# A fixed order, a PE run-up and later small loads for the first product of a decoder trunk

## The chip, the cores and the metric

The kernel runs on one core of one Trainium2 chip. The core has five engines that work side by side: TensorE (PE), which multiplies matrices and transposes tiles; VectorE (DVE); ScalarE (ACT); GpSimd (POOL); and SyncE (SP), which here only issues loads and stores. SyncE and ACT each have a DMA queue, and both share the core's 16 DMA engines. The metric is the device time of one execution in microseconds (us). The time before is the median of three runs.

## The reference

One layer of a hybrid decoder trunk on 256 tokens of 2048 channels in float32: a norm, one combined input projection, two token mixers side by side (a gated delta rule and a causal pooling), gates, an output projection, and a gated MLP with a causal convolution. What matters here is its beginning:

```
h = rmsnorm(x, norm_mix_w)                 # x: 256 x 2048
proj = h @ w_in                            # 2048 x 14368
q, k, v, z, b_raw, a_raw, p_in, g_a, g_b = split(proj)
qkv = silu(causal_dwconv(concat(q, k, v), conv_qkv_w))
```

The rest (delta rule, pooling, `w_out`, `w_up`, `w_down`, final norm) is not touched by the change.

## The kernel before

**Precision.** Every large product is done in three matmuls on split operands. ACT casts a float32 tile to the rounded type (`hi`), VectorE takes what is left (`lo`), and PE adds up hi x hi, lo x hi and hi x lo. The activations are the stationary operand, the weights the moving one.

**Weights.** `srcs` lists all weight tiles in the order of use, each 128 x 1024 (two blocks of 128 rows by 512 columns, 512 KB). `begin(n)` prepares tiles up to number n: a load on SyncE into one of four `raw` buffers (L110), the cast `whi` on ACT (L112), the rest `wlo` on VectorE (L119); `whi` and `wlo` have three buffers each. `weights()` prepares `AHEAD` = 2 tiles beyond the one that it hands out.

**Products.** `gemm_a` runs over the 8 weight tiles of a product (2048 rows). For each it does 12 matmuls, 128 x 128 by 128 x 512: two blocks, two halves of the tokens, three parts, at L149 (`xhi` with `whi`), L150 (`xlo` with `whi`) and L151 (`xhi` with `wlo`).

**The beginning.** x comes in four quarters `x0[c]` of 512 channels (L218), each followed by two weight tiles. The rows of `norm_mix_w` (`nmrows`) are turned on PE (L225) and copied to `nmw`. Then PE turns x in 128 x 128 blocks (L234, 8 transposes a quarter), and each turned block is scaled by `nmw` and split by ACT (`xhi`, L238) and VectorE (`xlo`, L239). The first product (`ps_k0`, the keys of the first heads) follows. The row norms of x are taken by squares on ACT (L311, 8 of 128 x 512) and are only needed when a product is evicted (L457). After the first product comes the small product for beta and decay (L362).

**Small loads.** ACT's queue loads `nmrows`, `vrows`, `cqrows`, `cfrows`, `alb`, `dtb`, `gwb`, `psb`, and writes four small blocks of zeros (L450). SyncE's queue loads the four `taps` of the value convolution (L466), which VectorE first reads at L476. The pooling bands are built on POOL and finished on VectorE by 8 subtractions (L430).

**Order.** The order of instructions on each engine is not written out: a planner lists them by priority (the order in the text) and by the time at which a simulated timeline has their inputs ready. Each engine then executes its list strictly in that order. Every DMA signals a semaphore when it has landed; there are eight of them in turn, over both queues, so an issue waits until the load that had the same semaphore before has landed.

```
 99     def weights():
101         begin(taken[0] + AHEAD + 1)
...
220         begin(2 * c + 2)
...
248     ps_k0 = gemm_a(xh, xl, KD)
```

Of the kernel before, what the change touches and what calls it, by code (L numbers as in the profile page):

```python
# [7 lines left out]
F32 = mybir.dt.float32  # L8
F32R = mybir.dt.float32r
I32 = mybir.dt.int32  # L10
AF = mybir.ActivationFunctionType
ALU = mybir.AluOpType

P = 128
S = 256
D = 2048
NH = 16
KD = D // P
DFF = 5632
KF = DFF // P  # L20
# [4 lines left out]
C_Q, C_K, C_V, C_Z = 0, 2048, 4096, 6144  # L25
# [3 lines left out]
AHEAD = 2  # L29
# [4 lines left out]
def kernel(  # L34
# [20 lines left out]
    nc = tc.nc  # L55
    mm = nc.tensor.matmul

    cpool = ctx.enter_context(tc.tile_pool(name="cpool", bufs=1))
    big = ctx.enter_context(tc.tile_pool(name="big", bufs=1))
    wpool = ctx.enter_context(tc.tile_pool(name="wpool", bufs=3))  # L60
# [6 lines left out]
    def nm(s):  # L67
        cnt[0] += 1
        return f"{s}_{cnt[0]}"

    def pg(shape=(P, 512)):
        return psg.tile(list(shape), F32, tag="g", name=nm("psg"))
# [6 lines left out]
    srcs = []  # L79
# [16 lines left out]
    made = []  # L96
    taken = [0]

    def weights():

        begin(taken[0] + AHEAD + 1)
        taken[0] += 1
        return made[taken[0] - 1]

    def begin(n):
        while len(made) < min(len(srcs), n):
            src = srcs[len(made)]
            shape = list(src.shape)
            raw = wpool.tile(shape, F32, tag="raw", name=nm("raw"), bufs=4)
            nc.sync.dma_start(raw, src)  # L110
            hi = wpool.tile(shape, F32R, tag="whi", name=nm("whi"))
            nc.scalar.copy(hi, raw)  # L112
            if shape[1] == 8:
                lo = None
                nc.vector.tensor_tensor(hi[:, :, 32:64], raw[:, :, 0:32], hi[:, :, 0:32].bitcast(F32),
                                        op=ALU.subtract)
            else:
                lo = wpool.tile(shape, F32R, tag="wlo", name=nm("wlo"))
                nc.vector.tensor_tensor(lo, raw, hi.bitcast(F32), op=ALU.subtract)  # L119
            made.append((hi, lo))  # L120
# [11 lines left out]
    def pm():  # L132
        return psm.tile([P, 2, 512], F32, tag="m", name=nm("psm"))
# [4 lines left out]
    def gemm_a(lh, ll, nk, steps=None, ps=None):  # L138

        ps = pm() if ps is None else ps  # L140
        for c in range(nk // 2) if steps is None else steps:
            if c == 1:
                while later:
                    later.pop(0)()
            hi, lo = weights()
            for kk in range(2):
                k = 2 * c + kk
                for t in range(2):
                    mm(ps[:, t, :], lh(k, t), hi[:, kk, :], start=(k == 0), stop=False)  # L149
                    mm(ps[:, t, :], ll(k, t), hi[:, kk, :], start=False, stop=False)  # L150
                    mm(ps[:, t, :], lh(k, t), lo[:, kk, :], start=False, stop=(k == nk - 1))  # L151
                side()
        return ps
# [45 lines left out]
    ones = cpool.tile([P, P], F32, name="ones")  # L199
    nc.gpsimd.memset(ones, 1.0)  # L200
    ident = cpool.tile([P, P], F32, name="ident")
# [2 lines left out]
    epsx = cpool.tile([P, 2], F32, name="epsx")  # L204
    nc.gpsimd.memset(epsx, -0.5)

    def mtile(i, shape, dt, name):
        return big.tile(shape, dt, tag=f"m{i}", name=name)

    mix = tc.tile_pool(name="mix", bufs=1)  # L210
    mp = mix.__enter__()

    nmrows = mp.tile([KD, P], F32, tag="w1", name="nmrows")
    nc.scalar.dma_start(nmrows, norm_mix_w[0].rearrange("(r p) -> r p", p=P))
    x0 = []
    for c in range(4):
        xc = mtile(c, [P, 2, 512], F32, f"x0_{c}")
        nc.sync.dma_start(xc, x[0, :, c * 512 : (c + 1) * 512].rearrange("(t p) d -> p t d", p=P))  # L218
        x0.append(xc)
        begin(2 * c + 2)  # L220


    nmw = cpool.tile([P, KD], F32, name="nmw")
    pv = pg()
    nc.tensor.transpose(pv[:, :KD], nmrows, ident[:KD, :KD])  # L225
    nc.vector.tensor_copy(nmw, pv[:, :KD])
    xhl = big.tile([P, KD, 2, S], F32R, tag="xhl", name="xhl")
    xhi, xlo = xhl[:, :, 0, :], xhl[:, :, 1, :]
    for k2 in range(KD // 2):
        pt = pg([P, 2, S])  # L230
        for kk in range(2):
            k = 2 * k2 + kk
            for t in range(2):
                nc.tensor.transpose(pt[:, kk, t * P : (t + 1) * P], x0[k // 4][:, t, (k % 4) * P : (k % 4 + 1) * P],  # L234
                                    ident)
        for kk in range(2):
            k = 2 * k2 + kk
            nc.scalar.activation(xhi[:, k, :], pt[:, kk, :], AF.Copy, scale=nmw[:, k : k + 1])  # L238
            nc.vector.scalar_tensor_tensor(xlo[:, k, :], pt[:, kk, :], nmw[:, k : k + 1], xhi[:, k, :].bitcast(F32),  # L239
                                           op0=ALU.mult, op1=ALU.subtract)  # L240

    def xh(k, t):
        return xhi[:, k, t * P : (t + 1) * P]
# [1 line left out]
    def xl(k, t):  # L245
        return xlo[:, k, t * P : (t + 1) * P]

    ps_k0 = gemm_a(xh, xl, KD)


    NV = 16 + KF
    V_FFN, V_CB = 0, 16
    vrows = mp.tile([NV, P], F32, tag="th", name="vrows")
    for off, n, src in ((V_FFN, 16, norm_ffn_w), (V_CB, KF, conv_ffn_b)):
        nc.scalar.dma_start(vrows[off : off + n, :], src[0].rearrange("(r p) -> r p", p=P))
    cqrows = mp.tile([96, 2, P], F32, tag="cy", bufs=2, name="cqrows")
    nc.scalar.dma_start(cqrows, conv_qkv_w.rearrange("o j (r p) -> (o j r) p", p=P)
                        .rearrange("(a q) p -> q a p", a=2))
    cfrows = mp.tile([66, 2, P], F32, tag="cy", bufs=2, name="cfrows")
    nc.scalar.dma_start(cfrows, conv_ffn_w.rearrange("o j (r p) -> (o j r) p", p=P)  # L260
                        .rearrange("(a q) p -> q a p", a=2))
    alb = cpool.tile([P, NH], F32, name="alb")
    nc.scalar.dma_start(alb, a_log[0].partition_broadcast(P))
    dtb = cpool.tile([P, NH], F32, name="dtb")
    nc.scalar.dma_start(dtb, dt_bias[0].partition_broadcast(P))

    vec = cpool.tile([P, NV], F32, name="vec")
    pv = pg()
# [3 lines left out]
    pv = pg()  # L272
# [4 lines left out]
    pv = pg()  # L277
# [3 lines left out]

    def scales(g):
        psb = mp.tile([P, 512], F32, tag="psb", name=nm("psb"))
        nc.scalar.dma_start(psb, pool_scale[0, 512 * g : 512 * g + 512].partition_broadcast(P))
        return psb

    gwb = mp.tile([P, P], F32, name="gwb")
    nc.scalar.dma_start(gwb, gdn_norm_w[0].partition_broadcast(P))

    def rstd_rows(ssq, dst):  # L290

# [12 lines left out]
        nc.vector.tensor_copy(dst, pr[:, :S])  # L304
        return rs

    ssq4 = cpool.tile([P, 2, 4], F32, tag="ssq4", name="ssq4a")
    for c in range(4):
        for t in range(2):
            junk = cpool.tile([P, 512], F32, tag="sqj", name=nm("junk"))  # L310
            nc.scalar.activation(junk, x0[c][:, t, :], AF.Square, accum_out=ssq4[:, t, c : c + 1])  # L311
    ssq = cpool.tile([P, 2], F32, name="ssq")
    nc.vector.tensor_reduce(ssq, ssq4, axis=mybir.AxisListType.X, op=ALU.add)
    rs1 = rstd_rows(ssq, None)
# [34 lines left out]
    idh = mp.tile([P, P], F32, name="idh")  # L349
# [8 lines left out]
    for c in range(2):  # L358
        hi, lo = weights()
        for kk in range(8):  # L360
            k = 8 * c + kk
# [57 lines left out]
    for g, win in enumerate(WINDOWS):  # L419
        bd = bands[:, g, :]  # L420
        nc.gpsimd.memset(bd, 0.5 / win)
        nc.vector.tensor_copy(bd[:, 0:PAD], icnt[:, g, :])
        for cs in (slice(0, P + PAD), slice(P + PAD, NB)):
            b = bd[:, cs]
            n = cs.stop - cs.start
            nc.gpsimd.affine_select(b, b, pattern=[[1, n]], compare_op=ALU.is_ge, fill=0.0, base=0,
                                    channel_multiplier=-1)
            nc.gpsimd.affine_select(b, b, pattern=[[-1, n]], compare_op=ALU.is_ge, fill=0.0, base=win - 1,
                                    channel_multiplier=1)
            nc.vector.tensor_tensor(b[:, 0:P], b[:, 0:P], idh, op=ALU.subtract)  # L430


    Ta = mp.tile([P, 8, P], F32, name="T")
# [11 lines left out]
    SH = 3  # L445
    vrow = dpool.tile([4, SH + S, 512], F32, tag="vrow", bufs=1, name="vrow")
    zr = mp.tile([P, 2, 512], F32, tag="mv", name="zr")
    nc.vector.memset(zr[:SH, 0, :], 0.0)
    for g in range(4):
        nc.scalar.dma_start(vrow[g, 0:SH, :], zr[:SH, 0, :])  # L450

    def evict(ps, by=None):

# [6 lines left out]
    def v_taps(g):  # L460

        taps = []
        for n, tag in enumerate(("sz", "yb")):
            tp = mp.tile([P, 2, 512], F32, tag=tag, name=nm("taps"))
            for i in range(2):
                nc.sync.dma_start(tp[:, i, :], conv_qkv_w[0, 2 * n + i, C_V + 512 * g : C_V + 512 * g + 512]  # L466
                                  .partition_broadcast(P))
                taps.append(tp[:, i, :].unsqueeze(1).to_broadcast([P, 2, 512]))
        taps_of[g] = taps

# [249 lines left out]
    for g in range(4):  # L720
# [17 lines left out]
        psb = scales(g)  # L738
# [77 lines left out]
    ssq4 = cpool.tile([P, 2, 4], F32, tag="ssq4", name="ssq4b")  # L816
    for c in range(4):
# [9 lines left out]
        for k2 in range(2):  # L827
            pt = pg([P, 2, S])
            for kk in range(2):
                k = 4 * c + 2 * k2 + kk  # L830
                for t in range(2):
                    nc.tensor.transpose(pt[:, kk, t * P : (t + 1) * P], xt[:, t, k * P : (k + 1) * P], ident)
            for kk in range(2):
                k = 4 * c + 2 * k2 + kk
# [13 lines left out]
    for c in range(DFF // 512):  # L848
# [4 lines left out]
        for f in range(4):  # L853
            r = 4 * c + f
# [97 lines left out]
```

## Time and profile before

| what | value |
|---|---|
| median of 3 runs | 1586.81 us (1585.77 to 1587.41) |
| profiled execution | 1584.99 us |
| its span (first to last instruction) | 1582.9 us |
| PE busy | 1561.9 us, 99% |
| VectorE, ACT busy | 1067.9 us (67%), 746.3 us (47%) |
| mean granted clock of PE | 0.997 |
| read from HBM | 297.56 MB, 191 GB/s over the span |
| first 15 us: PE busy in three stretches of 5 us | 0.25, 2.76, 4.18 us |

How to read it: the profile is one execution, and its own time is 1584.99 us, that is 2.09 us more than its span. PE is busy almost throughout; busy time of the other engines matters only where PE waits for them. In the timeline a row has start, length, engine, line, operation, output and inputs, and in brackets how long the engine stood idle before it and for what. The rows of matmuls overlap, so their pace is read from the starts. The chain of waits follows the work that ended last backwards; there a matmul's length is what it adds to the chain.

### The profile page before, as it was taken

The numbers are of one execution on the slowest core, as the hardware profiler recorded it, in microseconds if no ns is written. First come the engines' busy times: TensorE is split into PE (matmuls) and PEld (weight loads), VectorE is DVE, ScalarE is ACT, GpSimd is POOL, SyncE is SP. The second block draws the span as 40 slices with busy tenths as digits, with TensorE's granted clock in tenths as the row PEclk, the third lists the DMA queues.
The fourth block names the chain that finished last, engine by engine and source line by source line (L and its number), as shares of the span: only waits on it lengthen the run. The fifth ranks groups of instructions, "written<-read, shape, count | busy, mean of one in ns | idle before, by whom it ended". The sixth has DMA issues, their size and how long they took to land.

```text
span 1582.9 us, 21262 instructions
## 1 busy us (share of the span) xinstructions
PE 1561.9 (99%) x8052; PEld 1311.6 (83%) x8052; DVE 1067.9 (67%) x1619; ACT 746.3 (47%) x953; POOL 44.5 (3%) x69
## 2 busy tenths in 40 slices
PE   8999999999999999999999999999999999999997
PEld 6888888888878888788788888888888888888885
DVE  6798758885698757795555666666766667444445
ACT  6554435444555445544454544444444444333334
POOL 3010000000000000000000000000000000000000
PEclk9999999999999999999999999999999999999998
DMA  8667657776667757675556666666666666666664
GB/s 277 184 208 208 192 147 204 212 211 174 180 207 201 201 147 200 208 206 170 197 182 181 190 192 187 187 188 189 184 197 188 187 188 213 198 193 193 195 192 131
DMA packets 167924, 304.22 MB, mean 192 GB/s; under 512 B 19186, under 2 KB 22274, under 8 KB 167694
## 3 DMA queue, kind: packets, MB, share of 16 engines
q1 hardware_dynamic: 165088, 298.36, 63.9%
q10 hardware_dynamic: 2734, 4.51, 0.9%
q8 instruction: 63, 1.03, 0.2%
q14 instruction: 39, 0.32, 0.1%
HBM read 297.56 MB, written 5.27 MB: 191 GB/s over the span
## 4 chain that ended last, share of the span: by engine, by line
PE 96%; DVE 1%; DMA 1%; issue 1%; ACT 0%; SPq 0%; DVEq 0%; POOLq 0%; POOL 0%
PE psm L151 15%; PE psm L150 15%; PE psm L149 15%; PE psm L173 10%; PE psg L173 10%; PE psg L174 5%; PE psm L174 5%; PE psg L886 3%; PE psg L887 3%; PE psg L888 3%; PE psm L886 2%; PE psm L887 2%; PE psm L888 2%; PE psg L561 1%; PE psg L194 1%
## 5 line engine op out<-in xcount | busy, mean ns | idle before, releaser
L119 DVE TENSOR_TENSOR wlo<-raw,whi 128x1024 fp32r<-128x1024 f32 x528 | 645.6, 1224 | 424.2 <-ACT whi L112 415.7
L112 ACT CAST whi<-raw 128x1024 fp32r<-128x1024 f32 x530 | 557.7, 1053 | 746.0 <-PE psm L150 325.1
L149 PE MATMUL psm<-whi,xhl 128*128 128x512 f32 x896 | 352.3, 393 | 1.9 <-ACT xhl L238 1.9
L151 PE MATMUL psm<-wlo,xhl 128*128 128x512 f32 x896 | 352.6, 394 | 0.9 <-DVE wlo L119 0.9
L150 PE MATMUL psm<-whi,xhl 128*128 128x512 f32 x896 | 351.8, 393 | 0.0
L173 PE MATMUL psm<-fhl,whi 128*128 128x512 f32 x704 | 245.9, 396 | 0.0
L173 PE MATMUL psg<-fhl,whi 128*128 128x512 f32 x704 | 237.8, 394 | 0.0
L149 PEld LDWEIGHTS psm<-whi,xhl 128*128 128x128 f32 x896 | 168.6, 188 | 36.5 <-ACT xhl L238 2.3
L151 PEld LDWEIGHTS psm<-wlo,xhl 128*128 128x128 f32 x896 | 168.6, 188 | 35.9 <-DVE wlo L119 1.8
L150 PEld LDWEIGHTS psm<-whi,xhl 128*128 128x128 f32 x896 | 168.6, 188 | 34.7
L174 PE MATMUL psm<-fhl,wlo 128*128 128x256 f32 x704 | 194.2, 279 | 0.0
L174 PE MATMUL psg<-fhl,wlo 128*128 128x256 f32 x704 | 178.6, 279 | 0.0
L173 PEld LDWEIGHTS psm<-fhl,whi 128*128 128x128 f32 x704 | 131.4, 188 | 30.3
L173 PEld LDWEIGHTS psg<-fhl,whi 128*128 128x128 f32 x704 | 129.2, 188 | 24.0
L174 PEld LDWEIGHTS psg<-fhl,wlo 128*128 128x128 f32 x704 | 132.5, 188 | 6.9
L174 PEld LDWEIGHTS psm<-fhl,wlo 128*128 128x128 f32 x704 | 132.5, 188 | 1.1
L886 PE MATMUL psg<-whi,hhi 128*128 128x512 f32 x176 | 68.6, 390 | 0.0
L886 PE MATMUL psm<-whi,hhi 128*128 128x512 f32 x176 | 68.5, 389 | 0.0
L887 PE MATMUL psm<-whi,hlo 128*128 128x512 f32 x176 | 68.5, 389 | 0.0
L887 PE MATMUL psg<-whi,hlo 128*128 128x512 f32 x176 | 68.5, 389 | 0.0
L888 PE MATMUL psm<-wlo,hhi 128*128 128x512 f32 x176 | 68.5, 389 | 0.0
L888 PE MATMUL psg<-wlo,hhi 128*128 128x512 f32 x176 | 61.7, 389 | 0.0
(234 smaller groups left out, 1438.7 us busy)
## 6 DMA issues: line engine op xcount, KB each, us to landing
raw<-in_w_in_dram SPq DMA_DIRECT2D x226, 512.0 KB, 4.2
raw<-in_w_up_dram SPq DMA_DIRECT2D x176, 512.0 KB, 4.0
raw<-in_w_down_dram SPq DMA_DIRECT2D x88, 512.0 KB, 4.3
raw<-in_w_out_dram SPq DMA_DIRECT2D x32, 512.0 KB, 3.8
mv<-vrow SPq DMA_DIRECT2D x12, 512.0 KB, 5.4
taps<-in_conv_qkv_w_dram SPq DMA_DIRECT2D x16, 256.0 KB, 5.7
raw<-in_pool_w_dram SPq DMA_DIRECT2D x8, 512.0 KB, 5.0
x<-in_x_dram SPq DMA_DIRECT2D x4, 512.0 KB, 7.2
```

Source lines behind the costliest of these rows:

```text
L112: nc.scalar.copy(hi, raw)
L119: nc.vector.tensor_tensor(lo, raw, hi.bitcast(F32), op=ALU.subtract)
L149: mm(ps[:, t, :], lh(k, t), hi[:, kk, :], start=(k == 0), stop=False)
L150: mm(ps[:, t, :], ll(k, t), hi[:, kk, :], start=False, stop=False)
L151: mm(ps[:, t, :], lh(k, t), lo[:, kk, :], start=False, stop=(k == nk - 1))
L173: mm(ps[f], hi[:, kk, fs], rhl(k), start=(k == 0), stop=False, skip_group_check=True)
L174: mm(ps[f][:, 1, :], lo[:, kk, fs], rhl(k)[:, 0, :], start=False, stop=(k == nk - 1), skip_group_check=True)
L194: nc.tensor.transpose(pt[:, ff, t * P : (t + 1) * P], src[:, t, f * P : (f + 1) * P], ident)
L561: mm(pg0, kq[:, h, 0, 0:P], kq[:, h, :, :], start=True, stop=True)
L886: mm(acc[c][t], lh(k, t), hi[:, kk, :], start=(k == 0), stop=False)
L887: mm(acc[c][t], ll(k, t), hi[:, kk, :], start=False, stop=False)
L888: mm(acc[c][t], lh(k, t), lo[:, kk, :], start=False, stop=(k == KF - 1))
```

## The change

- The loads of weights are split off from their casts (`load` beside `begin`). At the beginning SyncE gets x and the first four weight tiles in the order x 0, weights 0 and 1, x 1, weights 2 and 3, x 2, x 3; the others come with their casts.
- A one-column copy on ACT (`first`) stands at the beginning, so that the activation table is loaded there. PE does 11 matmuls of ones with ones, 128 x 128, into a PSUM tile that nobody reads, and six more after the first quarter of x is turned.
- The first product is written out with a fixed order on PE, ACT and VectorE (`manual_schedule`; other instructions may still be placed between). A weight tile's 12 matmuls come as four `xhi` x `whi`, four `xlo` x `whi`, four `xhi` x `wlo`. The next quarter of x is turned after each even tile, one PSUM tile for each block of 128 channels; its parts alternate with the casts of the next two weight tiles. The casts run no longer `AHEAD`. The squares of x follow inside the same order.
- The small loads of ACT's queue but `nmrows` are queued behind the last x part on ACT (`issue_after(last_act)`), the band subtractions behind the last on VectorE, the taps behind the last weight load that has been written at that place.

```diff
@@ weights @@
-        begin(taken[0] + AHEAD + 1)
+        begin(taken[0] + ahead + 1)
+    def load(n):
+        while len(loads) < min(len(srcs), n):
+            raw = wpool.tile(list(src.shape), F32, tag="raw", name=nm("raw"), bufs=4)
+            last_load[0] = nc.sync.dma_start(raw, src).ins
+            loads.append(raw)
     def begin(n):
         while len(made) < min(len(srcs), n):
-            nc.sync.dma_start(raw, src)
+            load(len(made) + 1)
+            raw = loads[len(made)]
@@ beginning @@
+    first = cpool.tile([P, 1], F32, name="first")
+    nc.scalar.copy(first, ones[:, 0:1])
+    pr0 = pm()
+    def runup(n):
+        for _ in range(n):
+            mm(pr0[:, 0, :P], ones, ones, start=True, stop=True)
+    runup(11)
...
-        begin(2 * c + 2)
+        load(min(2 * c + 2, 4))
...
-    ps_k0 = gemm_a(xh, xl, KD)
+    def tile_k0(c):
+        hi, lo = weights(-1)
+        for w, part in ((hi, xh), (hi, xl), (lo, xh)):
+            for kk in range(2):
+                k = 2 * c + kk
+                for t in range(2):
+                    mm(ps_k0[:, t, :], part(k, t), w[:, kk, :], ...)
+    with tc.manual_schedule(engines={PE, DVE, Activation}):
+        pt = pg()
+        nc.tensor.transpose(pt[:, :KD], nmrows, ident[:KD, :KD])
+        nc.vector.tensor_copy(nmw, pt[:, :KD])
+        pts = turn_x(0)
+        runup(6)
+        parts_x(pts[:2])
+        begin(1)
+        parts_x(pts[2:])
+        begin(2)
+        for c in range(4):
+            tile_k0(2 * c)
+            if c < 3:
+                pts = turn_x(c + 1)
+                parts_x(pts[:2])
+                begin(2 * c + 3)
+                last_act, last_dve = parts_x(pts[2:])
+                begin(2 * c + 4)
+                square_x(c)
+            tile_k0(2 * c + 1)
+        square_x(3)
@@ small loads @@
+    with tc.issue_after(last_act):
+        # cqrows, alb, dtb, vrows (2), cfrows, gwb on ACT's queue; psb and vrow likewise
...
+            with tc.issue_after(last_dve):
+                nc.vector.tensor_tensor(b[:, 0:P], b[:, 0:P], idh, op=ALU.subtract)
...
+                with tc.issue_after(last_load[0]):
+                    nc.sync.dma_start(tp[:, i, :], conv_qkv_w[...])   # the taps
```

`turn_x(c)` holds the 8 transposes of a quarter, `parts_x` the operations of L238 and L239 for the turned blocks that it is given, `square_x(c)` the two squares of L311 for a quarter.

## The prediction

> **What bounds the kernel now.** I read the page first, then the timeline, the chain of waits and the list of waits of the first 80 us, since the diff touches only the first product and the loads around it. On the page:
>
> ```profile
> span 1582.9 us, 21262 instructions
> ...
> PE 1561.9 (99%) x8052; PEld 1311.6 (83%) x8052; DVE 1067.9 (67%) x1619; ACT 746.3 (47%) x953; POOL 44.5 (3%) x69
> ...
> PE 96%; DVE 1%; DMA 1%; issue 1%; ACT 0%; SPq 0%; DVEq 0%; POOLq 0%; POOL 0%
> ```
>
> TensorE (PE) sets the end. The PE work that the kernel needs stays as it is, so the change can gain only where PE stands still or runs slowly. PE idles 1582.9 - 1561.9 = 21.0 us. By the busy time in stretches, 7.8 us of it lie in the first 15 us (PE busy 0.25, 2.76 and 4.18 us of three 5 us stretches), 2.6 us from there to 800, nothing from 800 to 1560, and 10.7 us in the last 23 us. The gain has to come from the start. The timeline there:
>
> ```profile
> 0.78 0.20 POOL L200 MEMSET ones<- 128x128 f32 x1 [0.29 <-POOLq L936]
> ...
> 5.35 1.97 PE L234 MATMUL psg<-ident,x 128*128 128x128 f32 x8 [0.92 <-DMA x<-in_x_dram]
> ...
> 7.73 1.04 ACT L112 CAST whi<-raw 128x1024 fp32r<-128x1024 f32 x1 [0.77 <-DMA raw<-in_w_in_dram]
> ...
> 9.21 0.80 PE L149 MATMUL psm<-whi,xhl 128*128 128x512 f32 x1 [1.89 <-ACT xhl L238]
> ...
> 10.82 1.97 PE L234 MATMUL psg<-ident,x 128*128 128x128 f32 x8 [0.82 <-DMA x<-in_x_dram]
> ...
> 12.44 0.78 PE L150 MATMUL psm<-whi,xhl 128*128 128x512 f32 x1
> ```
>
> Weights and x for the first tile are ready at 9.2, but PE does one matmul and then stands at the transposes of the second x quarter, which the planner queued ahead of the rest and whose load lands at 10.8. The product runs from 12.44. The chain gives the pace (start, length, what):
>
> ```profile
> 14.07 0.43 PE psm L150
> 14.49 0.40 PE psm L151
> 14.89 0.23 PE psm L149
> 15.13 0.23 PE psm L150
> ...
> 19.49 0.87 PE psg L234 x8
> ...
> 37.74 0.23 PE psm L151
> ```
>
> Up to 14.5 a matmul takes 0.43 us, after that 0.23: the clock opens there, 3.9 us after dense work began at 10.82; eight transposes fall from 1.97 to 0.87. The open pace is exactly 0.227: L149 matmuls start at 50.29 and 59.81, 42 matmuls apart. A weight tile has 12 matmuls: 2.72 us.
>
> **The first product, step by step.** Eight tiles are 21.8 us. Before, its last matmul ends its turn at 37.8. Three transposes of small loads (L269, L274, L279) lie inside; by the spacings around them they cost 0.29 + 0.20 + 0.03 = 0.52 us, which the change only moves to later. So 37.3 is the time to beat.
>
> Start: tile 0 needs the cast of the first weight tile, which waited for its load until 7.73 and took 1.04: 8.8. The x parts no longer decide: the first two need x at 5.35, two transposes (0.5), and 2 x 0.47 on ACT: 6.8, before the weights land. Bounds: without small loads the weights could land up to 0.7 sooner (as long as that cast idled for them), but up to then ACT's queue moves 0.05 MB in 2.4% of the DMA time beside 1.37 MB of SyncE's queue (DMA view up to 7.7 us), 0.1 to 0.2 us of it, so I take nothing; late end 9.2, where the first matmul is now. In 8.8 + 21.8 + three quarter turns of 0.87 the product ends at 33.2: **4.1 us sooner** (3.7 to 4.9).
>
> Do the inputs keep up? Between a turn and the even tile after it PE has 0.87 + 2.72 = 3.6 us; ACT needs 0.3 for the first transposes, two parts (0.94) and a cast (1.05), 2.3 in all: cover 1.3 us. VectorE's wlo is then due 1.23 later, at 3.5, and is first read eight matmuls into the tile, at 5.4. The ACT load per pair of tiles is 4 x 0.47 + 2 x 1.05 + 2 x (0.63 + 0.19) = 5.6 us of 6.3; so squares now inside the product fit, by 0.7. Each wait in the fixed order has behind it the next cast on ACT and the next parts on VectorE, and PE waits for those; if a weight or x tile is over 1.3 us late, PE pays the rest at each of three seams. Transfers: landings come 1.3 to 2.4 us apart (x 5.3, weights 7.7 and 9.3, x 10.8, weights 12.1); the queue in its new order needs raw 2 at 12.5, x 2 at 17.8, raw 4 at about 19, and gives them near 12, 15 and 18. The PSUM slots of a turn are free when VectorE's last part is done, about 10.7, before PE turns at 11.5.
>
> Run-up: no trace has it. Nearest rows: 128-wide transposes at 0.246 closed and 0.109 open. Eleven take 1.2 to 2.7 us from 1.0 (ones are set at 0.98), so end by 3.7, before nmrows lets PE go at 4.18. Six take 0.7 to 1.5 after the turn at 5.35 to 7.3: at most 8.8, just where tile 0 starts. Cover gone (weights 0.7 sooner) it would cost up to 0.7. What it does to the clock: before, a lone spell of 1.97 us at 5.35 did not open it; 3.9 us of transposes and matmuls did. Now there are 2.7 us from 1.0, and an unbroken spell from 5.35 into the product. Counted as before, it opens at 9.25 at the latest, and 0.45 us of slow product lose 0.45 x (1 - 0.227/0.43) = **0.2 us**. Bounds 0 (the first spell opens it) to 1.8 (below).
>
> The Trainium skill, "TensorE: Matmul & The Clock Gate", Part 1, says that the clock opens after a busy window of some 3.4 us that runs free of the kernel, and Part 4 that transposes don't count as busy in the same way; by these the 2.7 us spell is too short, and the rest is the second rival. The opening at 14.5 to 14.7 fits both counts, as its last 2 us were matmuls and the spell that failed was all transposes.
>
> Table load: 1.28 us at 5.68 before; now hidden under the x load, which ends at 5.3. Kept late it would delay the first parts to about 8, still no later than the cast needs, so nothing either way. Transposes of nmrows, its copy: unchanged.
>
> Moved loads: twelve issues on ACT (cqrows, alb, dtb, two vrows, cfrows, gwb, psb, four zero rows) of 0.24 to 0.67 us each, 4.4 us in sum, go behind the last x part on ACT, which is near 27. The casts of tiles 7 to 10 and the squares are around them; cast 7 would be done at 28.2 and is due at 30.4, cover 2.2. On SyncE's queue, weight loads move past the taps, which VectorE first reads at 91.6 (L476) and which issue near 55. The eight band subtractions on VectorE (2.3 us) go behind 27 us, where it is idle over half of the time (busy 1.91 and 1.86 of 5 us from 30 to 40), and PE reads them near 126. I take 0, bounds below.
>
> Later order: the planner orders everything behind the manual part anew. The 2.6 us of idle between 15 and 800 is what it could win; as much it could lose. I take 0, and 2 us to both sides.
>
> **Sum:** 4.1 - 0.2 = 3.9 us. The profiled execution has 1584.99 us with its span of 1582.9 (2.09 around it), so 1579.0 and 1581.1 there. It lies 1.82 below the median of the runs, 1586.81; from the median, **1582.9**. About 0.2% (3.2 us) is what a measurement here can tell from no change.
>
> **Rivals.** (1) Slower: small loads hold ACT. An issue waits here until a load eight issues earlier has landed:
>
> ```profile
> 9.82 0.33 ACTq L288 DMA_DIRECT2D gwb<-in_gdn_norm_w_dram  x1
> ...
> 13.62 0.27 ACTq L450 DMA_DIRECT2D vrow<-zr  x1
> ...
> ACT whi L112 <- DMA alb<-in_a_log_dram: 0.9, 1, 0.9
> ```
>
> cqrows, issued at 2.46, had landed when gwb went out at 9.82, 7.4 us; alb, issued at 7.83, at 13.62, and a cast stood behind that. In the new place ACT has casts to make. A burst of twelve that wraps around the eight, at the zero rows' 0.26 us an issue, holds ACT 7.4 - 8 x 0.26 = 5.3 us; the cast behind it has 2.2 cover, so PE loses 3.1, and a second hold 5.3 in full: 3.9 - 8.4 = -4.5, 1591.3. It decides from 3.9 + 2.2 = 6.1 us of holding. Against: before, the planner had put other ACT work between the issues, and the two holds on record are 0.9 and 0.8. Chance 0.14.
>
> (2) The clock stays closed: only the product counts. From 8.8 it opens at 12.7, and 3.9 x 0.47 = 1.8 us are lost: gain 2.3, 1584.5, which reads as no change. If the six run-up matmuls count too, it opens at 11.2 and costs 1.1. For: eight transposes alone at 5.35 did not open it; against: in time, the dense spell ahead of 9.25 is as long as before. The skill's sentence above speaks for it. Chance 0.2.
>
> (3) The gain is given back later: one hold of rival 1, or a new later order. 0 to 1.5 us of gain, about 1586. For: VectorE is 0.97 busy in places (70 to 90, 100 to 120), so a shifted plan can make PE wait. Chance 0.1.
>
> (4) More: weights 0.7 sooner and the clock open at once: 4.9, and up to 1 later: 1581.4. Chance 0.06. It leaves 0.5 for the forecast, with its own range 1581.4 to 1584.4.
>
> **How the numbers follow.** Faster by over 0.2% (below 1583.6): the forecast but for 0.03, rival 4, and a little of 2: 0.55. Within: rivals 2 and 3, part of 1: 0.32. Slower (above 1590.0): most of rival 1: 0.13. The range goes from rival 4 with a lucky order, 1580.5, to 1588.0, past rivals 2 and 3; it leaves out rival 1's bad end and the far tail.
>
> **What would show it.** Right: the cast of the first weight tile near 7.7; first matmul of the product at 8.5 to 9.0; matmul spacing 0.23 from 9.3 on; PE back to back from there; the product's last matmul near 33; 75 to 160 us shifted by 4 us with nothing else. Wrong: spacing of 0.43 past 10 (rival 2); idle on PE after an ACT cast that waited for a small load between 27 and 40 (rival 1); idle at even tiles, waiting for ACT (cover too thin); a shift of 4 us at 40 that is smaller at 800 (rival 3).

## The result

The changed kernel takes 1581.95 us (median of 11 runs, 1581.01 to 1582.48), the kernel before 1586.11 beside it (11 runs). The ratio is 0.9975, with a 95% interval of 0.9967 to 0.9982: faster by 2.9 to 5.2 us. The profiled executions went from 1584.99 to 1581.20 us, their spans from 1582.9 to 1579.4. The forecast was 3.9 us less.

The page of the kernel after, the same three rows:

```profile
span 1579.4 us, 21330 instructions
...
PE 1565.1 (99%) x8086; PEld 1315.5 (83%) x8086; DVE 1066.2 (68%) x1619; ACT 745.4 (47%) x954; POOL 45.0 (3%) x69
...
PE 96%; DVE 1%; DMA 1%; issue 1%; ACT 0%; DVEq 0%; POOLq 0%; POOL 0%; SPq 0%
```

PE is still the bound; it is busier by 3.2 us, which is less than the 6.6 us that its run-ups take. The timeline of the kernel after (start, length, engine, line, what, idle time before it and its cause):

```profile
1.04 5.06 PE L222 MATMUL psm<-ones 128*128 128x128 f32 x22 [1.04 <-POOL ones L209]
...
6.25 1.16 PE L252 MATMUL psg<-ident,x 128*128 128x128 f32 x8
...
7.80 1.04 ACT L121 CAST whi<-raw 128x1024 fp32r<-128x1024 f32 x1 [0.17 <-DMA raw<-in_w_in_dram]
...
8.89 2.11 PE L285 MATMUL psm<-whi,xhl 128*128 128x512 f32 x8 [0.15 <-ACT whi L121]
```

The run-up comes first and is done when x is turned; the product starts at 8.89, as soon as the first weight tile is cast, and runs through. The chain of waits (start, length, what) has no stand from there to the small product (L418):

```profile
1.27 6.51 DMA raw<-in_w_in_dram
...
7.80 1.05 ACT whi L121
...
8.89 3.04 PE psm L285 x12
11.93 0.87 PE psg L252 x8
12.80 5.48 PE psm L285 x24
...
34.37 3.64 PE psg L418 x16
```

Load, cast, product: the run-up is not in the chain, and 12 matmuls take 3.04 us at once, 24 take 5.48: the clock is open from the first one. The trace's clock records put the opening at 6.42 us (before: 14.74).

For all that follows the mark is the start of the first matmul of the small product: 37.84 before, 34.21 after, **3.63 us sooner**. From the mark to the start of PE's last matmul both profiles have 1534.1 us, and from there to the end 11.0 and 11.1. So in these two profiles the whole gain is in the first product; nothing was won or lost later.

### The profile page after: what moved, and what is told of

It is laid out like the page before. It is cut to its first block, busy times and chain, and to the rows that moved or that the text cites. A ratio compares the mean times of both kernels' runs of the same rounds, so it can differ in the third digit from the quotient of the medians.

```text
span 1579.4 us, 21330 instructions
## 1 busy us (share of the span) xinstructions
PE 1565.1 (99%) x8086; PEld 1315.5 (83%) x8086; DVE 1066.2 (68%) x1619; ACT 745.4 (47%) x954; POOL 45.0 (3%) x69
## 3 DMA queue, kind: packets, MB, share of 16 engines
q8 instruction: 63, 1.03, 0.3%
## 4 chain that ended last, share of the span: by engine, by line
PE 96%; DVE 1%; DMA 1%; issue 1%; ACT 0%; DVEq 0%; POOLq 0%; POOL 0%; SPq 0%
PE psm L160 14%; PE psm L159 14%; PE psm L158 14%; PE psm L182 10%; PE psg L182 10%; PE psg L183 5%; PE psm L183 5%; PE psg L945 3%; PE psg L946 3%; PE psg L947 3%; PE psm L945 2%; PE psm L947 2%; PE psm L946 2%; PE psm L285 1%; PE psg L620 1%
## 5 line engine op out<-in xcount | busy, mean ns | idle before, releaser
L160 PE MATMUL psm<-wlo,xhl 128*128 128x512 f32 x864 | 339.5, 393 | 0.7 <-DVE wlo L128 0.7
L158 PE MATMUL psm<-whi,xhl 128*128 128x512 f32 x864 | 339.0, 392 | 0.0
L159 PE MATMUL psm<-whi,xhl 128*128 128x512 f32 x864 | 338.4, 392 | 0.0
L160 PEld LDWEIGHTS psm<-wlo,xhl 128*128 128x128 f32 x864 | 162.3, 188 | 34.3 <-DVE wlo L128 1.4
L159 PEld LDWEIGHTS psm<-whi,xhl 128*128 128x128 f32 x864 | 162.2, 188 | 33.4
L158 PEld LDWEIGHTS psm<-whi,xhl 128*128 128x128 f32 x864 | 162.3, 188 | 32.9 <-issue 0.2
```

## The experiments

Twelve kernels were run. "Opens" is the clock's first opening, "start" the first product's first matmul, "rest" the time from the mark to the start of PE's last matmul, all of one profile each, in us; the ratio is that of the times to the kernel before, with its interval.

| run | opens | start | mark | rest | ratio |
|---|---|---|---|---|---|
| before | 14.74 | 9.21 | 37.84 | 1534.1 | |
| after | 6.42 | 8.89 | 34.21 | 1534.1 | 0.9975 (0.9967 to 0.9982) |
| e1, after without run-ups | 11.78 | 8.78 | 35.45 | 1536.6 | 0.9996 (0.9987 to 1.0006) |
| e2, after with the planner's order | 6.08 | 9.10 | 35.76 | 1535.0 | 0.9984 (0.9975 to 0.9993) |
| e3, after with early small loads | 6.78 | 10.24 | 39.94 | 1533.9 | 1.0003 (0.9994 to 1.0012) |
| e4, before with a run-up | 6.95 | 9.19 | 39.10 | 1538.5 | 1.0003 (0.9993 to 1.0013) |
| e5, after, first run-up only | 4.39 | 8.92 | 34.21 | 1536.2 | 0.9987 (0.9977 to 0.9996) |
| e6, after, second run-up only | 9.93 | 9.54 | 35.15 | 1533.7 | 0.9982 (0.9973 to 0.9991) |
| e7, before with late small loads | 13.24 | 8.93 | 38.40 | 1533.5 | 0.9998 (0.9989 to 1.0008) |
| e8, after with the first tile in halves | 5.23 | 7.82 | 33.84 | 1533.3 | 0.9977 (0.9965 to 0.9988) |
| e9, e8 with later small transposes | 6.18 | 7.82 | 33.06 | 1536.4 | 0.9975 (0.9965 to 0.9985) |
| e10, e9 with a later solve (it did not move, see there) | 4.61 | 7.82 | 33.05 | 1535.9 | 0.9968 (0.9955 to 0.9980) |
| e11, after without the early table load | 4.42 | 9.89 | 35.24 | 1534.6 | one run, no ratio |
| e12, after with a first run-up of 6 | 9.61 | 9.60 | 35.21 | 1538.3 | 0.9987 (0.9978 to 0.9996) |

The intervals of the ratio are some 0.2% wide, 3 us. They set e1, e3, e4 and e7 apart from the kernel after (all four hold 1 and lie above its interval); they don't order the other variants, which is what the marks are for. Not taken away singly were the new order of loads on SyncE's queue, the later taps, the later band subtractions and the order of parts within a weight tile.

### One part taken away

**e1: both run-ups out.**

```diff
-    runup(11)
...
-        runup(6)
```

> The kernel after without both run-ups (11 and 6 matmuls of ones); order, loads and table load stay. The mark is the first matmul of the small product behind the first one: 37.84 us in the profile before, 34.21 after. Theory (the run-up buys the open clock): the product still starts near 8.9, since it waits for the first weight tile, but at 0.43 us a matmul until the clock opens, at the latest 3.9 us later; that costs up to 1.8 us, so the mark is near 36.0 and the time some 1583.8. Rival (the fixed order alone does it, as eight transposes and the product open the clock early anyway): spacing 0.23 from 9.5 on, mark 34.2 to 34.5, time as after.

The mark came at 35.45, the opening at 11.78. The first tile's first eight matmuls in the timeline show the closed clock:

```profile
8.78 3.48 PE L284 MATMUL psm<-whi,xhl 128*128 128x512 f32 x8 [1.01 <-ACT whi L121]
```

They take 3.48 us and not 2.11. The theory held: the run-up buys the open clock, worth 1.24 us in this profile, within the bound of 1.8 (how much it depends on the profile is said behind e12). The profile's rest is 2.5 us longer too; that is another matter (below, at e10).

**e2: order left to the planner.**

```diff
-    with tc.manual_schedule(engines={PE, DVE, Activation}):
+    with ExitStack():
```

> The kernel after with the order of the first product left to the planner; run-up, table load and late small loads stay. In the planner's list PE has the first transposes of the second x quarter behind two matmuls of the first tile. Theory (the order is worth the stall at those transposes): PE does two matmuls from 8.9, stands until that quarter has landed, near 10.4, and goes on at 0.23 us a matmul: 1.0 us lost, mark near 35.2, and some 0.3 more where transposes stand within tiles. Rival A (run-up does it all): mark 34.2 to 34.4. Rival B (the order is nearly all of the gain): mark over 36.5.

Mark 35.76, so the order is worth 1.55 us: more than the 1.0 of the theory, less than rival B. The place was right (timeline):

```profile
9.10 0.73 PE L285 MATMUL psm<-whi,xhl 128*128 128x512 f32 x2 [0.43 <-ACT xhl L258]
...
10.42 0.41 PE L252 MATMUL psg<-ident,x 128*128 128x128 f32 x2 [0.59 <-DVE xhl L259]
```

PE does two matmuls and stands. The profile names VectorE's last part of the quarter before, which frees the PSUM slot at 10.34, but the second quarter of x landed at 10.29, so the reason of the theory would have held PE just as long. Counted between starts of matmuls, this stand costs 0.8 us, a second one up to 11.91, again behind VectorE's parts, 0.3, and the later start 0.2; that is 1.3 of the 1.55.

**e3: the small loads at the beginning again.**

```diff
-    with tc.issue_after(last_act):     # three places, twelve loads
+    with ExitStack():
```

> The kernel after with the twelve small loads of ACT's queue no longer queued behind the last x part, so that the planner puts them at the beginning again; everything else stays. Theory of the prediction (they are hidden there): the first weight tile lands at most 0.2 us later, mark 34.2 to 34.5. Rival (in the fixed order each of them that waits for a landing holds the casts): the first cast or a part of x waits 0.9 us or more for a small load, the product starts at 9.8 or later, mark 35.1 to 37.

The prediction's theory failed here: mark 39.94, 5.73 later, more than the rival's price, and the whole gain of the change is gone. The list of waits of the first 42 us (who for whom: us in total, times, longest) names it:

```profile
ACT xhl L258 <- DMA vrows<-in_conv_ffn_b_dram: 5.7, 1, 5.7
ACT xhl L258 <- DMA vrow<-zr: 5.5, 1, 5.5
...
PE psm L285 <- ACT whi L121: 3.7, 2, 2.4
```

Twice small issues stood on ACT until earlier loads with the same semaphores had landed: the second part of `vrows` until 7.76, when `cqrows` was in, with the first x parts behind it; and the four zero rows, which got out between 13.16 and 16.76, with the second quarter's parts behind them. In the second stand PE was idle for 2.4 us and slow afterwards: the clock records show it closed from 20.43 to 23.84.

**e11: no early table load.**

```diff
-    first = cpool.tile([P, 1], F32, name="first")
-    nc.scalar.copy(first, ones[:, 0:1])
```

> The kernel after without the one-column copy on ACT. Theory: the table load is then placed ahead of the first x part, behind the issue for nmrows, and runs at 1.3 us as well, since nothing holds ACT there any more; start 8.9, mark 34.2. Rival (the load waits with the first x part and takes its 1.28 us after the turn): first x part at 7.5 or later, first cast at 9, mark 35.4.

The rival was right. In the list ACT has the table load ahead of the first x part, but it ran with it (timeline):

```profile
6.77 1.28 ACT L256 ACT_TABLE_LOAD   x1 [6.77 <-DVE nmw L289]
...
8.07 0.84 ACT L256 ACTIVATE xhl<-psg,nmw 128x256 fp32r<-128x256 f32 x2
...
8.80 1.04 ACT L121 CAST whi<-raw 128x1024 fp32r<-128x1024 f32 x1
```

The load waited for `nmw` like the part itself, and the first cast, behind both on ACT, ran at 8.80 and not at 7.80. Mark 35.24: worth 1.03 us.

### One part alone, on the kernel before

**e4: the run-up and the table load.**

```diff
+    nc.scalar.copy(first, ones[:, 0:1])
+    for _ in range(11):
+        mm(pr0[:, 0, :P], ones, ones, start=True, stop=True)
```

> The kernel before with the 11 run-up matmuls and the early table load and nothing else of the change. In the profile after these 11 take 5.06 us (two passes each, 22 records), to 6.1, and the clock opens at the end of them. Theory (the clock stays open over the gap): the transposes at 10.8 take 0.9 us and not 1.97, and six matmuls 0.23 and not 0.43: 2.3 us saved, mark 35.5. Rival (PE has only eight transposes and one matmul between 6.1 and 10.8, so the clock closes again): spacing 0.43 at 12.5 as before, mark 37.5 to 37.9, nothing saved.

The rival held, and more: 1.26 us later than before. The clock opened at 6.95, closed at 10.36 after a stretch with eight transposes and one matmul, and opened again only at 17.19 (timeline):

```profile
9.19 0.49 PE L149 MATMUL psm<-whi,xhl 128*128 128x512 f32 x1 [1.53 <-ACT xhl L244]
...
11.09 1.97 PE L240 MATMUL psg<-ident,x 128*128 128x128 f32 x8 [1.40 <-DMA x<-in_x_dram]
```

The transposes at 11.09 take 1.97 us again. Here the run-up was worth nothing, since the order left PE idle after it.

**e7: the late small loads.**

```diff
+    with tc.issue_after(last_act):     # the same twelve loads
```

> The kernel before with only the twelve small loads of ACT's queue put behind the last x part; no run-up, no fixed order. Theory of the prediction (the loads at the beginning cost the first cast at most 0.2 us): start of the product as before but for 0.2, mark 37.4 to 37.9. Rival (the planner's list changes with them: ACT and PE are listed differently when ACT is not held, and PE now has seven matmuls of the first tile ahead of the second quarter's transposes): the product runs from 8.8 at the closed clock without the stand until 12.4, opens near 12.5, mark 35.5 to 36.5.

Neither: mark 38.40, 0.56 later than before. The product started at 8.93 and passed the second quarter, as the rival had it, but behind that its casts waited, 3.1 us for weights and, behind the late issues, 4.3 us (the list of waits from 8 to 40 us):

```profile
ACT whi L112 <- DMA vrows<-in_norm_ffn_w_dram: 4.3, 2, 2.2
ACT whi L112 <- DMA raw<-in_w_in_dram: 3.1, 2, 2.5
...
PE psg L275 <- DMA cqrows<-in_conv_qkv_w_dram: 0.9, 1, 0.9
...
PE psm L151 <- DVE wlo L119: 0.5, 1, 0.5
```

So late issues do hold casts, as rival 1 of the prediction had it, here in the planner's order. What PE itself paid were two other stands: 0.5 us for a `wlo` whose weights came late, and 0.9 us at the transposes of `cqrows`, which had not landed. What the held casts alone would have cost is not shown. And the first seven matmuls took 3.6 us at the closed clock, until 12.5, where the open clock takes 1.6.

### The run-up's length and its second half

**e5: the six out.** `runup(6)` removed.

> The kernel after with the first run-up (11) and without the second (6). The mark is again the first matmul of the small product: 34.21 after, 35.45 with neither run-up. In the run with a run-up added to the kernel before, the clock opened at 6.95 and closed one window later, at 10.36, with PE mostly idle between. Theory (the six keep the clock open over the wait for the weights): PE is idle from 7.2 to 8.9, the window that begins where the clock opens holds 0.7 us of transposes and 0.9 of product, so it closes near 9.8, stays closed for at least 3.4 us and costs 1.6: mark 35.8, worse than with neither. Rival (1.7 us of idleness is too short to close it): mark 34.2.

The rival held: mark 34.21, the 1.7 us of idleness ahead of the product didn't close the clock. In this run it had opened early, at 4.39; whether the six help when the opening falls otherwise was not tried (more on this behind e12).

**e6: the eleven out.** `runup(11)` removed.

> The kernel after with the second run-up (6) and without the first (11). Theory (six matmuls behind the turn give an unbroken spell from 5.35, but late): the turn takes 1.97 at the closed clock, the 12 records of the six 2.6 us more, so PE reaches the product at 9.9 and not 8.9, with the clock opening between 8.8 and 12.2; mark 35.2 to 36.3. Rival (this spell alone opens the clock in time, the eleven are idle work): opening before 8.9 and mark 34.2 to 34.5.

The theory held, at the lower end of its range (mark 35.15, opening 9.93): the turn at the closed clock and six run-up matmuls of 2.56 us fill the chain until 9.9.

**e12: six and not eleven.** `runup(11)` became `runup(6)`.

> The kernel after with a first run-up of 6 and not 11: 2.6 us of it, to 3.6, the length that the prediction took for the eleven. Theory (the opening needs a window of 3.4 us that is nearly full; the spell from 1.04 is now too short for any): the clock opens only with the second spell, from 5.35 on, between 8.8 and 10; the turn and the six run at the closed clock and end at 9.5 to 9.9; mark 34.9 to 35.3 as with the second run-up alone (35.15). Rival (2.6 us suffice, as the prediction took it): opening before 6.9, start 8.9, mark 34.2.

The theory held. The first spell ended by 4.0 and opened nothing; the opening came at 9.61, with the turn and the second run-up slow (timeline):

```profile
5.42 1.97 PE L252 MATMUL psg<-ident,x 128*128 128x128 f32 x8 [1.18 <-DMA x<-in_x_dram]
...
7.19 2.66 PE L222 MATMUL psm<-ones 128*128 128x128 f32 x12
```

**The clock over all fourteen profiles.** Within a run, all openings and closings are whole multiples of 3.41 us apart (e12: 9.61, 313.39, 316.81). Where these moments lie differs from profile to profile: with the same eleven run-up matmuls the first opening falls between 4.39 and 6.95 (nine profiles), in all of them ahead of the product. Between such moments lie windows of 3.41 us, and the idle time of PE in a window (transposes counted as busy) goes with what the clock does at its end, the kernel's last 20 us left out:

| the clock at the end of a window | idle time of PE in the window |
|---|---|
| opens | 0 to 0.41 us |
| stays closed | 0.72 us or more |
| stays open | at most 1.43 us |
| closes (e3, e4 twice, e12) | 1.94 to 2.29 us |

This answers e5: its idleness fell into two windows, which end at 7.80 and 11.22 and have 1.06 and 1.11 us of idle time each; the same 1.7 us in one window lies where no profile decides. It also says what a mark is worth. In e1 the window that opened the clock began at 8.37, 0.41 us ahead of the product; where the windows lie otherwise, the opening can come up to one window later and cost up to 3.41 x (1 - 0.227/0.43) = 1.6 us more (an estimate from the two paces). So 1.24 us is the price of that one profile, and the same holds for the marks of e4, e6, e7, e12 and of the kernel before. That the ten runs of e1 keep nothing of the gain (0.9996), where its mark keeps 2.4 of the 3.63 us, fits this but is not traced.

### A version meant to beat both

**e8: first weight tile in halves** (load, cast and rest in two blocks; matmuls block by block; two matmuls in the second run-up).

```diff
+        begin_half(0)
+        parts_x(pts[1:2])
+        begin_half(1)
-        runup(6)
+        runup(2)
```

> A version meant to beat the kernel after: the first weight tile is loaded, cast and split in two halves, the first x part goes before the first half and the second between, the first tile's matmuls go block by block, and the second run-up has two matmuls and not six, since it would end at 8.7. Theory (the start waits for the landing and the cast of a whole tile, 7.8 + 1.04): the first half lands near 7.0, its cast of 0.55 ends near 7.9 behind the first x part, PE starts at 7.9, mark 33.2, span 1 us shorter. Rival A (landings do not come in order, the half lands no earlier than 7.6): start 8.3, mark 33.6. Rival B (without the other four run-up matmuls the clock closes): spacing 0.43 from some point before 12, mark over 34.5.

The start came as the theory had it (7.82), and 48 matmuls later the product was still 1.09 ahead (20.64 against 21.73), but the mark only 0.37. The timeline shows what took the rest, with idle time of PE before it:

```profile
32.71 0.31 PE L359 MATMUL psg<-ident,cfrows 66*128 66x66 f32 x2 [0.53 <-DMA cfrows<-in_conv_ffn_w_dram]
```

**e9: those transposes behind the last tile.**

```diff
+    with tc.issue_after(last_pe[0]):
         nc.tensor.transpose(pv[:, :NV], vrows, ident[:NV, :NV])   # cqrows, cfrows likewise
```

> The version with the first weight tile in halves, with one edit more: the five transposes of the small loads (vrows, cqrows, cfrows) are queued on PE behind the first product's last matmul. In the run with halves alone the product started at 7.82, 1.07 us sooner than after, but the mark came only 0.37 sooner (33.84), as PE stood at one of these transposes until cfrows had landed, inside the last tile. Theory (that stand ate the rest): the transposes are late enough to find their loads landed, mark 33.1 to 33.3, span 1.0 to 1.1 below the one after. Rival (the casts of the small product's tiles are late instead, which the stand only hid): mark 33.6 to 33.9.

Mark 33.06, 1.15 sooner than after; for the mark the theory held. But the span grew (1580.5), as this profile's rest is 2.3 us longer, and the times give the same ratio as after. The version is sooner at the mark; that it is faster as a whole is not shown.

**e10: the block solve four steps later.**

```diff
-        for _ in range(WAIT):
+        for _ in range(WAIT + 4):
```

> The version before this one, and VectorE starts the block solve of each head group four steps later (nine and not five; a step is 6 matmuls, 1.36 us). From the mark to the last matmul the profiles have 1533.3 to 1538.4 us; the longer ones have one or two stands of 2 us at a wlo that waits on VectorE behind the solve's first multiplication, which waits 4.6 to 6.7 us for the block load. Theory (these stands make the scatter between runs and between variants): with nine steps no wait of that multiplication over 1 us, the stretch from the mark 1533.0 to 1534.2, times closer together, and a median some 1 us lower than without. Rival (the stands come from late weight loads and any instruction would wait): the same scatter, and nothing gained; or later steps of the solve collide and PE waits when the group ends, slower by 1 to 5 us.

The edit did not do what it was meant to. Semaphore instructions left out, PE, VectorE, GpSimd and SyncE run through the same list of operations and tiles in e9 and e10; only on ACT seven places near the start differ. So the solve did not start later, its first multiplication still waited 5.3 us for the block load, and the theory was not tested. That the planner's simulated landing decides VectorE's order, whatever the step, is a guess. The ratio of e10 is the lowest, but its interval holds the 0.9975 of e9, and with the same order on VectorE and PE the difference is noise.

What the stands are can be read from the traces all the same. The timeline of e9 at one of them:

```profile
308.51 0.42 DVE L686 TENSOR_TENSOR tmp<-lb,tb 128x248 f32<-128x248 f32 x1 [6.05 <-DMA lb<-cdd]
...
309.56 1.04 ACT L125 CAST whi<-raw 128x1024 fp32r<-128x1024 f32 x1 [2.32 <-DMA raw<-in_w_in_dram]
309.74 1.22 DVE L132 TENSOR_TENSOR wlo<-raw,whi 128x1024 fp32r<-128x1024 f32 x1
...
311.01 0.50 PE L174 MATMUL psm<-wlo,xhl 128*128 128x512 f32 x1 [1.71 <-DVE wlo L132]
```

PE stands for the `wlo` that VectorE starts at 309.74. The cast at 309.56, which waited for late weights, is still running then, so this `wlo` belongs to another tile; by the semaphore that both wait for, to the one cast at 303.42. It stood behind the solve's multiplication, which waited for the block load until 308.51. That is the mechanism of the theory, not of the rival. Over the fourteen profiles it fits: in seven, PE stands 0.9 to 2.6 us (between starts of matmuls) near 310 or 490, and there the multiplication waited 5.1 to 6.7 us; behind its other waits, of up to 4.7 us, PE stood at most 0.5 us. In e4 and e12, whose rests are the longest, the clock also closed for 3.41 us right behind the stand. All this makes the rest vary by 5 us and hides differences of 1 us between variants. Why the block load lands late in some runs only is left open, and no kernel here takes the wait away.

## Why the prediction was right

- **Start.** 8.8 expected, 8.89 measured. The load landed as before (cast at 7.80 and 7.73), so taking nothing for the queue's relief was right.
- **Product.** 96 matmuls took 22.2 us by the chain and not 21.8, the three turns 2.6 as worked out, the small transposes 0.64 and not 0.52. With the 0.1 at the start, 0.6 of the 4.1 us is gone; the clock's 0.2 was not lost. That leaves 3.5, and the mark shows 3.63 for the 3.9 of the sum. By the starts in both timelines, nearly all of it are 0.3 us at the start, 2.1 at the stand (9.21 to 12.44 for one matmul and a turn, which take 1.1 at the open clock) and 1.1 in the five matmuls at the closed clock behind it. The casts were in time at all three seams: in the timeline the first matmuls behind each turn show no idle time.
- **Run-up: right in the result, wrong in a term.** Eleven were sized at 1.2 to 2.7 us by transposes; they took 5.06 us. A float32 matmul of ones is two records of 0.213 at the closed clock, where a transpose is one of 0.246. So PE turned x at 6.25 and not 5.35, which the weights' landing hid with only 0.17 us to spare at the cast. And the clock did not open late in the second spell (9.25) but at 6.42 in the first, because that was twice as long. With the length that the prediction took, e12 shows 35.21: not the 0.2 us of the sum but 1.0, as the turn runs at the closed clock and the six run-up matmuls, 2.66 us there and not 1.5, hold the product until 9.60. So it was luck that the eleven opened the clock in time: they did because they were twice as long as the sum had them. The Trainium skill, "TensorE: Matmul & The Clock Gate", Part 1, has openings after a busy window of some 3.4 us, and these windows run free of the kernel. The trace agrees: closings and openings within one run are 3.41 us apart or a multiple of that (20.43 to 23.84; 6.95, 10.36 and 17.19), and the first spell of e12, 2.6 us, opened nothing. Whether transposes count for it was not told apart.
- **Table load: a term put at nothing that was not nothing.** "Nothing either way" costed the first parts alone; on ACT the cast stands behind them, and e11 paid 1.03 us.
- **Moved loads: the sum right, the reason incomplete.** They win nothing by themselves (e7), and in the new place none of the twelve held a cast: 25.71 to 32.80, spread between casts and squares. But the prediction priced leaving them at the start at 0.1 to 0.2 us; in the fixed order it is 5.73 (e3), by the mechanism of rival 1, at the old place and not at the new one.
- **Later order.** 0 expected, 0 measured: 1534.1 and 1534.1. That is one profile each, and both happen to be without the stands described at e10; in e4 the rest is 4.4 us longer.

The parts do not add up. Taken away singly, run-up, order, late loads and table load cost 1.24, 1.55, 5.73 and 1.03 us, 9.55 in sum, of a gain of 3.63; alone on the kernel before, run-up (with the early table load) and late loads cost 1.26 and 0.56 us. Each of the four parts taken away lets a wait or a slow spell back in that eats gain of the others.

## What to carry to other kernels

Read from the chain which load the first matmul waits for, and arrange everything else to be done by then; a warm clock is worth something only if the order keeps PE busy from the run-up into the product. On a queue that also computes, a DMA issue that waits for a semaphore costs what stands behind it, so place small loads where the engine has nothing due. Compare variants of such a start at a mark inside the trace, as single late loads elsewhere change the total by more than the parts of the start are worth; and look where the clock's windows lie in each profile before taking a difference of 1 us for the variant's. Before a result is explained, see in the trace that the edit moved what it was to move (e10).

## What was not expected of the hardware

A float32 matmul of 128 x 128 with ones shows as two records (22 for 11, 0.213 us each at the closed clock), a transpose of the same size as one (0.246). A table load waits like the instruction that it is for (e11: 6.77 us idle for `nmw`, though nothing else held ACT). A clock opened by a run-up closed again 3.41 us later over a stretch with eight transposes and one matmul (e4; 2.2 us of idle time in that window), but not over 1.7 us of idleness that two windows shared (e5).
